# Pinning the low-part subtracts and the norms' short steps on VectorE, and looping a token-major projection over weights first

## The chip, the cores and the metric

The kernel runs on one NeuronCore of a Trainium2 chip. The time is the device time of one execution in microseconds; the number given is the median of several. The engines of the core that matter here are TensorE (PE in the profile; PEld is its weight load), VectorE (DVE), ScalarE (ACT), and the DMA queue that SyncE (SP) issues to. Each engine works through its own list of instructions in order; an instruction that waits for another engine holds up what stands behind it on its own.

## The reference

Two layers of a decoder trunk on 256 tokens with a width of 1024, all in float32. `h` is the running state, and every stage begins with an RMS norm of it.

```python
for i in range(DEPTH):                                    # DEPTH = 2
    h = h + 0.5 * swiglu(rmsnorm(h, ffn1_norm[i]), ffn1_w_gate[i], ffn1_w_up[i], ffn1_w_down[i])
    u = rmsnorm(h, mix_norm[i])
    (q, c_kv, q_idx, w_idx, k_idx, x_pool, z, xbc, dt_raw, gate_raw) = jnp.split(u @ w_in[i], offs, axis=-1)
    y_attn = dsa_attention(q, rmsnorm(c_kv, kv_norm[i]), q_idx, w_idx,
                           rmsnorm(k_idx, idx_k_norm[i]), w_uk[i], w_uv[i])
    y_pool = pool_mixer(x_pool, pool_w[i], pool_scale[i])
    y_ssd = ssd_mixer(z, xbc, dt_raw, ...)                # ends in an RMS norm too
    g_attn, g_pool, g_ssd = jnp.split(jax.nn.sigmoid(gate_raw), N_BRANCHES, axis=-1)
    h = h + (g_attn * (y_attn @ w_br_attn[i]) + g_pool * (y_pool @ w_br_pool[i])
             + g_ssd * (y_ssd @ w_br_ssd[i])) @ w_out[i]
    h = h + 0.5 * swiglu(rmsnorm(h, ffn2_norm[i]), ffn2_w_gate[i], ffn2_w_up[i], ffn2_w_down[i])
    h = h + jax.nn.sigmoid(rmsnorm(h, ple_norm[i]) @ ple_w_gate[i]) * (p[i] @ ple_w_proj[i])
return rmsnorm(h, final_norm)
```

with `rmsnorm(x, g) = x * rsqrt(mean(x*x) + EPS) * g` and `swiglu(x, g, u, d) = (silu(x @ g) * (x @ u)) @ d`. D_FF is 2816.

## The kernel before

**Products.** `h` is kept with the feature on the 128 partitions, as 8 chunks of 128 x 256 tokens. Each float32 matrix product is made of three matmuls of rounded parts (`mm3`): high of the weight by high of the state, high by low, and low by high. The parts of the state are `uh` and `ul` (`gh` and `gl` inside a feed-forward), those of the weight `whi` and `wlo`.

**Weight units.** Weights come in units of 128 x 1024 (512 KB). For each, SP issues one DMA into a `raw` buffer, ACT casts it to `whi` (L136) and DVE subtracts to get `wlo` (L137). There are four `raw` buffers and five each of `whi` and `wlo`; `unit` loads four units ahead of the one in use. So the DMA of a unit waits for the `wlo` subtract four units earlier, and the cast of a unit waits for the last matmul that reads the unit five earlier. A unit is read by 24 matmuls, except the four units `BF0` to `BF3` of the token-major part (below), which are 128 x 704 each.

**Norms.** A stage begins its matmuls on the state times the norm's gain, without the norm's factor, which is a number for each token. Meanwhile `rnorm` works out the factor: a matmul with ones over the sum of squares (L106), `rs_v` (L242), a seed and three Newton rounds on 128 x 2 numbers (L188 to L202), then the factor on a diagonal in two parts, `dh` and `dl` (L247, L248), then two matmuls with ones (L106, out of `t,onesr`), which spread it over the partitions, and an ACT copy to `rs_r` (L257). The stage's later steps (`later()`) pull the next piece of this; `gap` counts how many such pulls lie between the diagonal and the two matmuls. The results of the first matmuls are multiplied by `rs_r` as they leave their banks: in a feed-forward at L354, in the mixer at L440.

**The mixer's start.** `mix` first makes a token-major product (the units `BF0` to `BF3` are the moving side, the two halves of 128 tokens the stationary side; results in two `aux` banks; the outer loop runs over the token halves), then four index-query units `IN20` to `IN23` on the state without the norm's factor, with L440 behind them. Everything after needs the normed state: DVE makes it chunk by chunk (L449), ACT rounds it to `uh` (L175) and DVE subtracts to `ul` (L176). A second, separate norm (128 x 4 numbers, `v4` and `rk`) belongs to the attention's latent and keys.

**Order.** A list scheduler sets the order of the instructions on each engine by its own estimate of when each is ready. Matmuls are kept in program order. Everything else is free, apart from true dependences; the norm's steps have a raised priority.

## Time and profile before

| what | value |
|---|---|
| time, three runs | 1350.65, 1351.76, 1351.86 us; median 1351.76 us |
| the profiled execution: its own time | 1352.77 us |
| the profiled execution: span of the core | 1351.0 us |
| PE busy | 1316.8 us, 97% of the span |
| DVE busy | 1041.8 us, 77% |
| ACT busy | 742.8 us, 55% |
| `wlo` subtracts (L137) | 457, mean 1215 ns |
| casts to `whi` (L136) | 457, mean 1045 ns |
| weight DMA of 512 KB, issue to landing | 447, median 3.8 us |

The span runs from the first to the last instruction that the profile shows, and the execution's own time is 1.8 us longer. A share of busy time is a mean over all stages. TensorE's clock has two levels, 1.2 and 2.4 GHz; a granted clock of 1.00 in a stretch is the upper one throughout.

### The profile page before, as it was taken

The numbers are of one execution on the slowest core, as the hardware profiler recorded it, in microseconds if no ns is written. First come the engines' busy times: TensorE is split into PE (matmuls) and PEld (weight loads), VectorE is DVE, ScalarE is ACT, GpSimd is POOL, SyncE is SP. The second block draws the span as 40 slices with busy tenths as digits, with TensorE's granted clock in tenths as the row PEclk, the third lists the DMA queues.
The fourth block names the chain that finished last, engine by engine and source line by source line (L and its number), as shares of the span: only waits on it lengthen the run. The fifth ranks groups of instructions, "written<-read, shape, count | busy, mean of one in ns | idle before, by whom it ended". The sixth has DMA issues, their size and how long they took to land.

```text
span 1351.0 us, 28294 instructions
## 1 busy us (share of the span) xinstructions
PE 1316.8 (97%) x11502; PEld 1304.2 (97%) x11502; DVE 1041.8 (77%) x1971; ACT 742.8 (55%) x1209; POOL 3.4 (0%) x17
## 2 busy tenths in 40 slices
PE   7999998999999999999989999989999999999997
PEld 7999998999999999999979999989999999999997
DVE  6877658987989777766877776679789887777666
ACT  5545445656864555545545444456577646545454
POOL 0000000000000000000000000000000000000000
PEclk9999998999999999999989999989999999999999
DMA  7666645556546565666545656545565565566661
GB/s 256 196 195 192 197 155 173 179 184 206 171 155 197 194 199 190 196 193 193 190 134 189 198 191 195 167 153 171 194 197 178 171 196 192 188 198 190 196 193 48
DMA packets 72386, 248.24 MB, mean 184 GB/s; under 512 B 7937, under 2 KB 10305, under 8 KB 72257
## 3 DMA queue, kind: packets, MB, share of 16 engines
q1 hardware_dynamic: 71392, 245.17, 56.5%
q8 instruction: 90, 1.47, 0.4%
q10 hardware_dynamic: 864, 1.28, 0.3%
q14 instruction: 40, 0.32, 0.1%
HBM read 245.33 MB, written 1.08 MB: 182 GB/s over the span
## 4 chain that ended last, share of the span: by engine, by line
PE 93%; DVE 2%; DMA 1%; issue 1%; ACT 1%; SPq 0%; DVEq 0%; ACTq 0%
PE mm L159 29%; PE mm L161 29%; PE mm L160 29%; PE aux L106 3%; DMA raw<-in_w_dram 1%; ACT whi L136 1%; DVE wlo L137 1%; PE aux L109 1%; PE aux L160 1%; PE aux L159 1%; PE aux L161 1%; DMA h<-in_x_dram 0%; DVE t L449 0%; DVE rs_t L200 0%; ACT uh L179 0%
## 5 line engine op out<-in xcount | busy, mean ns | idle before, releaser
L136 ACT CAST whi<-raw 128x1024 fp32r<-128x1024 f32 (+1 forms) x457 | 475.9, 1045 | 504.2 <-issue 247.3
L159 PE MATMUL mm<-uh,whi 128*128 128x256 f32 x2560 | 714.1, 280 | 12.9 <-ACT whi L153 6.3
L137 DVE TENSOR_TENSOR wlo<-raw,whi 128x1024 fp32r<-128x1024 f32 (+1 forms) x457 | 554.4, 1215 | 219.2 <-ACT whi L136 215.2
L160 PE MATMUL mm<-ul,whi 128*128 128x256 f32 x2560 | 712.3, 279 | 6.7 <-DVE ul L176 6.7
L161 PE MATMUL mm<-uh,wlo 128*128 128x256 f32 x2560 | 711.7, 279 | 0.0
L159 PEld LDWEIGHTS mm<-uh,whi 128*128 128x128 f32 x2560 | 483.5, 190 | 17.8 <-ACT whi L153 6.3
L160 PEld LDWEIGHTS mm<-ul,whi 128*128 128x128 f32 x2560 | 485.8, 190 | 7.4 <-DVE ul L176 7.1
L161 PEld LDWEIGHTS mm<-uh,wlo 128*128 128x128 f32 x2560 | 485.1, 190 | 0.6 <-DVE wlo L154 0.2
L161 PE MATMUL mm<-gh,wlo 128*128 128x256 f32 x704 | 194.1, 276 | 0.0
L160 PE MATMUL mm<-gl,whi 128*128 128x256 f32 x704 | 194.1, 276 | 0.0
L159 PE MATMUL mm<-gh,whi 128*128 128x256 f32 x704 | 193.7, 276 | 0.0
L160 PEld LDWEIGHTS mm<-gl,whi 128*128 128x128 f32 x704 | 132.1, 188 | 0.0
L161 PEld LDWEIGHTS mm<-gh,wlo 128*128 128x128 f32 x704 | 132.1, 188 | 0.0
L159 PEld LDWEIGHTS mm<-gh,whi 128*128 128x128 f32 x704 | 131.8, 188 | 0.0
L159 PE MATMUL mm<-a,whi 128*128 128x256 f32 x256 | 70.5, 277 | 0.0
L161 PE MATMUL mm<-a,wlo 128*128 128x256 f32 x256 | 70.4, 276 | 0.0
L160 PE MATMUL mm<-a,whi 128*128 128x256 f32 x256 | 70.4, 276 | 0.0
L160 PEld LDWEIGHTS mm<-a,whi 128*128 128x128 f32 x256 | 47.9, 188 | 0.0
L159 PEld LDWEIGHTS mm<-a,whi 128*128 128x128 f32 x256 | 47.9, 188 | 0.0
L161 PEld LDWEIGHTS mm<-a,wlo 128*128 128x128 f32 x256 | 47.9, 188 | 0.0
L354 DVE TENSOR_TENSOR t<-mm,rs_r 128x256 f32<-128x256 f32 x88 | 37.3, 423 | 12.8 <-ACT rs_r L257 2.5
L359 DVE SCALAR_TENSOR_TENSOR t<-t,t 128x256 f32<-128x256 f32 x88 | 37.4, 425 | 3.1
(209 smaller groups left out, 1097.6 us busy)
## 6 DMA issues: line engine op xcount, KB each, us to landing
raw<-in_w_dram SPq DMA_DIRECT2D x447, 512.0 KB, 3.8
gh<-rates SPq DMA_DIRECT2D x16, 256.0 KB, 4.2
raw<-in_w_dram SPq DMA_DIRECT2D x8, 352.0 KB, 2.9
raw<-in_w_dram SPq DMA_DIRECT2D x4, 256.0 KB, 3.6
gh<-rates SPq DMA_DIRECT2D x8, 128.0 KB, 3.5
h<-in_x_dram SPq DMA_DIRECT2D x2, 256.0 KB, 3.9
h<-in_x_dram SPq DMA_DIRECT2D x1, 512.0 KB, 6.7
t<-in_p_dram ACTq DMA_DIRECT2D x2, 256.0 KB, 5.7
```

Source lines behind the costliest of these rows:

```text
L106: self.tc.keep_in_program_order(self.nc.tensor.matmul(*args, **kw))
L109: self.tc.keep_in_program_order(self.nc.tensor.transpose(*args))
L136: nc.scalar.copy(hi[:, :n], raw[:, :n])
L137: nc.vector.tensor_tensor(lo[:, :n], raw[:, :n], hi[:, :n].bitcast(F), op=OP.subtract)
L159: mm(ps, a[0], b[0], start=start, stop=False)
L160: mm(ps, a[0], b[1], start=False, stop=False)
L161: mm(ps, a[1], b[0], start=False, stop=stop)
L354: nc.vector.tensor_tensor(t, p1[0], r, op=OP.mult)
L359: nc.vector.scalar_tensor_tensor(g, th, 1.0, t, op0=OP.add, op1=OP.mult)
```

## The change

Three things are edited.

- `turn` gives an instruction a token, and all instructions with this token keep on their engine the order in which the program issues them. It goes on every `wlo` subtract made in `load`, and on the norms' short steps: `rs_v`, the rsqrt's steps, `dh` and `dl`. In the rsqrt of 4 numbers two of the steps in each round go without. So a `wlo` subtract can't move across such a step any more in either direction; other DVE work can still stand between.
- In the feed-forwards `gap` is 2 where it was 3, except in the kernel's first.
- In `mix` the token-major product loops over the four units outside and over the two token halves inside. The pulls of the norm's steps come after the second, third and fourth unit.

```diff
--- before.py
+++ after.py
@@ -109,6 +109,10 @@
         self.tc.keep_in_program_order(self.nc.tensor.transpose(*args))
 
 
+    def turn(self, ins):
+        self.tc.stamp_issue_order_token(ins.ins, "turn")
+
+
     AHEAD = 4
 
     def unit(self, *key):
@@ -134,7 +138,8 @@
         raw, hi, lo = self.parts()
         nc.sync.dma_start(raw[:, :n], self.ins["w"][layer, u, :, :n])
         nc.scalar.copy(hi[:, :n], raw[:, :n])
-        nc.vector.tensor_tensor(lo[:, :n], raw[:, :n], hi[:, :n].bitcast(F), op=OP.subtract)
+        self.turn(nc.vector.tensor_tensor(lo[:, :n], raw[:, :n], hi[:, :n].bitcast(F),
+                                          op=OP.subtract))
         return hi, lo
 
     def first(self, c):
@@ -185,11 +190,11 @@
         nc = self.nc
         xh = self.t([P, 8], tag="rs_h", bufs=2)
         t = self.t([P, 8], tag="rs_t", bufs=2)
-        nc.vector.tensor_scalar(t[:, :n].bitcast(I32), x.bitcast(I32), 1, None,
-                                op0=OP.logical_shift_right)
-        nc.vector.tensor_scalar(xh[:, :n], x, -0.5, None, op0=OP.mult)
-        nc.vector.tensor_scalar(y[:, :n].bitcast(I32), t[:, :n].bitcast(I32), -1, 0x5F3759DF,
-                                op0=OP.mult, op1=OP.add)
+        self.turn(nc.vector.tensor_scalar(t[:, :n].bitcast(I32), x.bitcast(I32), 1, None,
+                                          op0=OP.logical_shift_right))
+        self.turn(nc.vector.tensor_scalar(xh[:, :n], x, -0.5, None, op0=OP.mult))
+        self.turn(nc.vector.tensor_scalar(y[:, :n].bitcast(I32), t[:, :n].bitcast(I32), -1,
+                                          0x5F3759DF, op0=OP.mult, op1=OP.add))
         for _ in range(3):
             if n > 2:
                 nc.vector.tensor_tensor(t[:, :n], y[:, :n], xh[:, :n], op=OP.mult)
@@ -197,10 +202,10 @@
             else:
                 for i in range(n):
                     s = slice(i, i + 1)
-                    nc.vector.scalar_tensor_tensor(t[:, s], y[:, s], xh[:, s], y[:, s],
-                                                   op0=OP.mult, op1=OP.mult)
-            nc.vector.scalar_tensor_tensor(y[:, :n], t[:, :n], 1.5, y[:, :n],
-                                           op0=OP.add, op1=OP.mult)
+                    self.turn(nc.vector.scalar_tensor_tensor(t[:, s], y[:, s], xh[:, s],
+                                                             y[:, s], op0=OP.mult, op1=OP.mult))
+            self.turn(nc.vector.scalar_tensor_tensor(y[:, :n], t[:, :n], 1.5, y[:, :n],
+                                                     op0=OP.add, op1=OP.mult))
 
     def square(self, c, src, add=True):
 
@@ -239,14 +244,16 @@
                 for h in range(2):
                     self.mm(ps[:, h:h + 1], acc[:, h * P:(h + 1) * P], self.ones[:, :1],
                                      start=True, stop=True)
-                nc.vector.tensor_scalar(v, ps[:, :2], 1.0 / D, EPS, op0=OP.mult, op1=OP.add)
+                self.turn(nc.vector.tensor_scalar(v, ps[:, :2], 1.0 / D, EPS, op0=OP.mult,
+                                                  op1=OP.add))
                 self.rsqrt(rc, v, 2)
                 dh, dl = (self.t([P, 2, P], FR, tag="t1") for _ in range(2))
                 for h in range(2):
                     x = rc[:, h:h + 1]
-                    nc.vector.tensor_scalar(dh[:, h], self.ident, x, None, op0=OP.mult)
-                    nc.vector.scalar_tensor_tensor(dl[:, h], self.ident, x, dh[:, h].bitcast(F),
-                                                   op0=OP.mult, op1=OP.subtract)
+                    self.turn(nc.vector.tensor_scalar(dh[:, h], self.ident, x, None, op0=OP.mult))
+                    self.turn(nc.vector.scalar_tensor_tensor(dl[:, h], self.ident, x,
+                                                             dh[:, h].bitcast(F), op0=OP.mult,
+                                                             op1=OP.subtract))
             for _ in range(gap):
                 yield
             pr = self.bank("aux")
@@ -330,7 +337,7 @@
     def ffn(self, layer, u0, nxt):
         nc = self.nc
         first = layer == 0 and u0 == U_FFN1
-        _, r = self.rnorm(late=first, gap=3)
+        _, r = self.rnorm(late=first, gap=3 if first else 2)
         gh = self.a([P, KF, S], FR, "gh")
         gl = self.a([P, KF, S], FR, "gl")
         waiting = []
@@ -398,7 +405,6 @@
         u0 = self.uh, self.ul
 
 
-        wu = [self.unit(layer, U_BF + i, 2 * BF) for i in range(4)]
 
         big1 = self.a([P, KF, S], F, "gh")
         big2 = self.a([P, KF, S], F, "gl")
@@ -410,18 +416,17 @@
         sm = self.a([P, 2, 96], F, "sm")[:, :, :88]
         ki2 = self.t([P, 2, 2, 64], tag="t1")
         ss = self.t([P, 4], tag="ss", bufs=1)
-        pb = []
-        for h in range(2):
-            ts = slice(h * P, (h + 1) * P)
-            ps = self.bank("aux")
-            for k in range(KD):
-                w = wu[k // 2]
-                s = slice((k % 2) * BF, (k % 2) * BF + 344)
-                self.mm3(ps[:, :344], (u0[0][:, k, ts], u0[1][:, k, ts]),
-                         (w[0][:, s], w[1][:, s]), k == 0, k == KD - 1)
-                if k % 4 == 3:
-                    self.later()
-            pb.append(ps)
+        pb = [self.bank("aux") for _ in range(2)]
+        for i in range(4):
+            w = self.unit(layer, U_BF + i, 2 * BF)
+            for h in range(2):
+                ts = slice(h * P, (h + 1) * P)
+                for k in (2 * i, 2 * i + 1):
+                    s = slice((k % 2) * BF, (k % 2) * BF + 344)
+                    self.mm3(pb[h][:, :344], (u0[0][:, k, ts], u0[1][:, k, ts]),
+                             (w[0][:, s], w[1][:, s]), k == 0, k == KD - 1)
+            if i > 0:
+                self.later()
         for h, ps in enumerate(pb):
             nc.scalar.mul(cn[:, h], ps[:, :256], rc[:, h:h + 1])
             nc.scalar.mul(sm[:, h], ps[:, 256:344], rc[:, h:h + 1])
```

The number of matmuls, casts and subtracts and the order of the DMA issues stay as they were. Three places of the order on the engines follow. (Line numbers of the kernel after are higher by 4 to 7: L137 is L141, L200 to L202 are L205 to L207, L247 and L248 are L253 and L254, L354 is L361.)

First DVE at the start of layer 0's mixer. The norm's steps are `rs_t`, `rs_y` and the two `t` out of `ident`; `wlo_2488`, `wlo_2494`, `wlo_2500` and `wlo_2604` are the units `IN21`, `IN22`, `IN23` and `IN0`. Before:

```order
L200 SCALAR_TENSOR_TENSOR rs_t_2527<-rs_y_2479,rs_h_2526 128x1 x2
L137 TENSOR_TENSOR wlo_2488<-raw_2486,whi_2487 128x1024
L202 SCALAR_TENSOR_TENSOR rs_y_2479<-rs_t_2527,rs_y_2479 128x2
L137 TENSOR_TENSOR wlo_2494<-raw_2492,whi_2493 128x1024
L247 TENSOR_SCALAR t_372_2540<-ident,rs_y_2479 128x128 x2
L137 TENSOR_TENSOR wlo_2500<-raw_2498,whi_2499 128x1024
L137 TENSOR_TENSOR wlo_2604<-raw_2602,whi_2603 128x1024
L248 SCALAR_TENSOR_TENSOR t_373_2541<-ident,rs_y_2479,t_372_2540 128x128 x2
L794 TENSOR_TENSOR dt_x_3904<-sm_2506,cc_93 128x32
```

And after; `wlo_2549`, `wlo_2567` and `wlo_2604` are `IN22`, `IN23` and `IN0`, and `wlo_2634` is `IN32`:

```order
L205 SCALAR_TENSOR_TENSOR rs_t_2528<-rs_y_2479,rs_h_2527 128x1 x2
L207 SCALAR_TENSOR_TENSOR rs_y_2479<-rs_t_2528,rs_y_2479 128x2
L253 TENSOR_SCALAR t_367_2541<-ident,rs_y_2479 128x128
L254 SCALAR_TENSOR_TENSOR t_368_2542<-ident,rs_y_2479,t_367_2541 128x128
L253 TENSOR_SCALAR t_367_2541<-ident,rs_y_2479 128x128
L254 SCALAR_TENSOR_TENSOR t_368_2542<-ident,rs_y_2479,t_367_2541 128x128
L141 TENSOR_TENSOR wlo_2549<-raw_2547,whi_2548 128x1024
L141 TENSOR_TENSOR wlo_2567<-raw_2565,whi_2566 128x1024
L141 TENSOR_TENSOR wlo_2604<-raw_2602,whi_2603 128x1024
L799 TENSOR_TENSOR dt_x_3904<-sm_2482,cc_93 128x32
L468 TENSOR_SCALAR v_414_2771<-ss_2484 128x2
L141 TENSOR_TENSOR wlo_2634<-raw_2632,whi_2633 128x1024
```

Four subtracts stood inside the norm's steps; now that of `IN21` stands ahead of `rs_v` (not shown) and the others behind the last diagonal step. Farther on, the subtracts of the next two units, `IN1` and `IN2`, stand between the six L449 (now L454) and the first L176 (now L181); before, they stood ahead of L440, and that of `IN3` stood where they are now.

Second PE in the token-major part of layer 0: `aux_2509` and `aux_2558` are the banks of the two token halves before, `whi_2341` and `wlo_2342` are unit `BF0`, `whi_2440` is `BF3`, `mm_2601` takes `IN20`. Before, from the last matmul of the first half to the first three of the second:

```order
L161 MATMUL aux_2509<-whi_2440,ul_1745 128x344
L159 MATMUL mm_2601<-uh_1744,whi_2481 128x256
L160 MATMUL mm_2601<-ul_1745,whi_2481 128x256
L106 MATMUL aux_2522<-ones,acc_1836 128x1 x2
L159 MATMUL aux_2558<-whi_2341,uh_1744 128x344
L160 MATMUL aux_2558<-wlo_2342,uh_1744 128x344
L161 MATMUL aux_2558<-whi_2341,ul_1745 128x344
```

And after, from the fourth matmul of the part on; `aux_2485` and `aux_2486` are the banks of the halves:

```order
L164 MATMUL aux_2485<-whi_2341,uh_1744 128x344
L165 MATMUL aux_2485<-wlo_2342,uh_1744 128x344
L166 MATMUL aux_2485<-whi_2341,ul_1745 128x344
L164 MATMUL aux_2486<-whi_2341,uh_1744 128x344
L165 MATMUL aux_2486<-wlo_2342,uh_1744 128x344
L166 MATMUL aux_2486<-whi_2341,ul_1745 128x344
L164 MATMUL aux_2486<-whi_2341,uh_1744 128x344
```

The second half's matmuls on `BF0` stood behind all of the first half; now they are the seventh to the twelfth matmul of the part. The matmul of ones over the sum of squares stood behind 24 of the part's 48 matmuls and 17 matmuls on `IN20`; now it stands behind 40 of the 48 and none on `IN20`.

Third DVE at the start of layer 1's first feed-forward. `wlo_8954` and `wlo_8984` are its units `F1_6` and `F1_7`, the next two are `F1_8` and `F1_9`, and `wlo_9107` is `F1_10`. Before:

```order
L242 TENSOR_SCALAR rs_v_8861<-aux_8927 128x2
L137 TENSOR_TENSOR wlo_8954<-raw_8952,whi_8953 128x1024
L188 TENSOR_SCALAR rs_t_8932<-rs_v_8861 128x2
L190 TENSOR_SCALAR rs_h_8931<-rs_v_8861 128x2
L137 TENSOR_TENSOR wlo_8984<-raw_8982,whi_8983 128x1024
L191 TENSOR_SCALAR rs_y_8862<-rs_t_8932 128x2
L137 TENSOR_TENSOR wlo_9015<-raw_9013,whi_9014 128x1024
L200 SCALAR_TENSOR_TENSOR rs_t_8932<-rs_y_8862,rs_h_8931 128x1 x2
L137 TENSOR_TENSOR wlo_9049<-raw_9047,whi_9048 128x1024
L202 SCALAR_TENSOR_TENSOR rs_y_8862<-rs_t_8932,rs_y_8862 128x2
L137 TENSOR_TENSOR wlo_9107<-raw_9105,whi_9106 128x1024
L200 SCALAR_TENSOR_TENSOR rs_t_8932<-rs_y_8862,rs_h_8931 128x1 x2
```

And after, from the third Newton round on:

```order
L205 SCALAR_TENSOR_TENSOR rs_t_8932<-rs_y_8862,rs_h_8931 128x1 x2
L207 SCALAR_TENSOR_TENSOR rs_y_8862<-rs_t_8932,rs_y_8862 128x2
L253 TENSOR_SCALAR t_1309_8945<-ident,rs_y_8862 128x128
L254 SCALAR_TENSOR_TENSOR t_1310_8946<-ident,rs_y_8862,t_1309_8945 128x128
L253 TENSOR_SCALAR t_1309_8945<-ident,rs_y_8862 128x128
L254 SCALAR_TENSOR_TENSOR t_1310_8946<-ident,rs_y_8862,t_1309_8945 128x128
L141 TENSOR_TENSOR wlo_8954<-raw_8952,whi_8953 128x1024
L141 TENSOR_TENSOR wlo_8984<-raw_8982,whi_8983 128x1024
L141 TENSOR_TENSOR wlo_9037<-raw_9035,whi_9036 128x1024
L141 TENSOR_TENSOR wlo_9067<-raw_9065,whi_9066 128x1024
L361 TENSOR_TENSOR t_1319_9016<-mm_8865,rs_r_8860 128x256
L141 TENSOR_TENSOR wlo_9107<-raw_9105,whi_9106 128x1024
```

The subtracts of `F1_6` to `F1_10` stood singly between the norm's steps; now the steps from `rs_v` to the last diagonal step stand in one piece, four subtracts follow, and then comes the first L361 (before: L354).

## Rows read from the trace of the kernel before

**Rows 1.** The page: span; busy us, share and instructions of each engine.
```profile
span 1351.0 us, 28294 instructions
...
PE 1316.8 (97%) x11502; PEld 1304.2 (97%) x11502; DVE 1041.8 (77%) x1971; ACT 742.8 (55%) x1209; POOL 3.4 (0%) x17
```

**Rows 2.** Windows: length, busy PE, PEld, DVE, ACT, POOL, PEclk, DMA share, GB/s.
```profile
200.00:240.00 40.00, 34.36 (x282) 33.83 (x281) 32.62 (x78) 24.53 (x45) 0.00 (x0) 0.91 0.51 169
219.00:230.00 11.00, 10.87 (x80) 10.87 (x81) 7.29 (x23) 3.46 (x6) 0.00 (x0) 0.83 0.24 73
240.00:300.00 60.00, 60.00 (x545) 59.67 (x544) 56.00 (x135) 37.94 (x59) 0.59 (x2) 1.00 0.55 173
887.00:898.00 11.00, 11.00 (x78) 11.00 (x79) 6.69 (x22) 3.21 (x6) 0.00 (x0) 0.78 0.19 63
```

**Rows 3.** PE timeline, mixer of layer 0: start, us, instruction, [idle before <-releaser].
```profile
212.60 0.28 PE L161 MATMUL mm<-uh,wlo 128*128 128x256 f32 x1
214.97 0.62 PE L159 MATMUL mm<-uh,whi 128*128 128x256 f32 x3 [2.10 <-ACT uh L175]
219.13 0.58 PE L160 MATMUL mm<-ul,whi 128*128 128x256 f32 x1 [3.54 <-DVE ul L176]
219.51 0.41 PE L161 MATMUL mm<-uh,wlo 128*128 128x256 f32 x1
```

**Rows 4.** Timeline of PE, start of the token-major part of layer 0.
```profile
193.49 0.32 PE L159 MATMUL aux<-whi,uh 128*128 128x344 f32 x1
193.65 0.32 PE L160 MATMUL aux<-wlo,uh 128*128 128x344 f32 x1
```

**Rows 5.** Timeline of ACT, start of layer 0's mixer.
```profile
200.88 3.90 ACT L136 CAST whi<-raw 128x1024 fp32r<-128x1024 f32 x4 [5.45 <-issue]
...
211.93 0.37 ACT L257 COPY rs_r<-aux 128x256 f32<-128x256 f32 x1
```

**Rows 6.** Timeline of DVE, start of layer 0's mixer.
```profile
199.78 0.16 DVE L242 TENSOR_SCALAR rs_v<-aux 128x2 f32<-128x2 f32 x1 [3.12 <-PE aux L106]
...
201.96 1.23 DVE L137 TENSOR_TENSOR wlo<-raw,whi 128x1024 fp32r<-128x1024 f32 x1
...
204.31 0.48 DVE L247 TENSOR_SCALAR t<-ident,rs_y 128x128 fp32r<-128x128 f32 x2
204.70 2.36 DVE L137 TENSOR_TENSOR wlo<-raw,whi 128x1024 fp32r<-128x1024 f32 x2
206.97 0.61 DVE L248 SCALAR_TENSOR_TENSOR t<-ident,rs_y,t 128x128 fp32r<-128x128 f32 x2
...
213.88 2.46 DVE L449 SCALAR_TENSOR_TENSOR t<-h,cc,rs_r 128x256 f32<-128x256 f32 x6
...
216.92 1.22 DVE L137 TENSOR_TENSOR wlo<-raw,whi 128x1024 fp32r<-128x1024 f32 x1
...
218.66 1.09 DVE L176 TENSOR_TENSOR ul<-t,uh 128x256 fp32r<-128x256 f32 x3
```

**Rows 7.** Timeline of PE, start of layer 1's mixer.
```profile
883.00 0.62 PE L159 MATMUL mm<-uh,whi 128*128 128x256 f32 x3 [1.85 <-ACT uh L175]
886.79 0.58 PE L160 MATMUL mm<-ul,whi 128*128 128x256 f32 x1 [3.17 <-DVE ul L176]
```

**Rows 8.** Timeline of PE, start of layer 1's first feed-forward.
```profile
688.52 0.28 PE L161 MATMUL mm<-uh,wlo 128*128 128x256 f32 x1
694.55 1.01 PE L106 MATMUL aux<-t,onesr 128*128 128x256 f32 x2 [5.76 <-DVE t L247]
696.49 0.58 PE L159 MATMUL mm<-uh,whi 128*128 128x256 f32 x1 [0.92 <-DVE t L354]
```

**Rows 9.** Timeline of DVE, start of layer 1's first feed-forward.
```profile
684.33 0.15 DVE L242 TENSOR_SCALAR rs_v<-aux 128x2 f32<-128x2 f32 x1
...
691.63 1.22 DVE L137 TENSOR_TENSOR wlo<-raw,whi 128x1024 fp32r<-128x1024 f32 x1 [1.28 <-ACT whi L136]
...
696.01 0.42 DVE L354 TENSOR_TENSOR t<-mm,rs_r 128x256 f32<-128x256 f32 x1 [1.08 <-ACT rs_r L257]
```

## The prediction

> **What bounds the kernel now.** The page comes first: PE is busy for 1316.8 of 1351.0 us [rows 1]. So only PE's idle time and the time in which it runs at the lower clock can be won. Second come windows of PE's busy time along the span: they are full except in seven places: the start and the end of the kernel, which no edit touches, a small gap at each second feed-forward, and three larger ones, at the start of layer 0's mixer (34.36 of 40 us, clock 0.91 [rows 2]), of layer 1's first feed-forward and of layer 1's mixer. Third, PE's timeline there, where the reader is to see the gaps and their releasers.
>
> In layer 0's mixer PE stops after the matmul at 212.60, runs three at 214.97, and waits 3.54 us more, for `ul`, till 219.13 [rows 3]. At 219.51 a matmul takes 0.41 us where 0.28 is usual, and the granted clock from 219 to 230 is 0.83 [rows 2, 3]: 17% of 11 us, 1.9 us, is lost on top of 5.6 idle. Layer 1's mixer shows the same shape: restarts at 883.00 and 886.79, idle 1.85 and 3.17 [rows 7], then a clock of 0.78 over 11 us, 2.4 us lost [rows 2]. In the feed-forward PE stops after 688.52, is idle 5.76 before the two spreading matmuls and 0.92 behind them, and starts anew at 696.49 [rows 8]. Fourth, who is late: DVE and ACT. In the mixer four `wlo` subtracts run between the first Newton round and the last diagonal step: `rs_v` is at 199.78, L248 only at 206.97 [rows 6]; ACT stood still for 5.45 us and then casts four units in a row at 200.88 [rows 5], because it waited for the buffers of the `BF` units, whose last reader was the second token half.
>
> **The change, part by part.**
>
> *Loop order.* A token-major matmul starts 0.16 us after the one ahead [rows 4]. `BF0` is released after 12 of them, 193.49 + 12 x 0.16 = 195.4; the casts of `IN21` to `IN0` then run from there as units come free (one every 1.9 us), in time ACT spent idle, and are done by 202.5 instead of 204.8. No instruction is added. The price: the ones matmul stands behind 40 of them, 193.49 + 40 x 0.16 = 199.9, so `rs_v` comes at about 200.4 instead of 199.78, 0.6 later.
>
> *Pins, mixer of layer 0.* From `rs_v` to the first subtract between is 2.2 us [rows 6]; one L202 (0.2) and four diagonal steps (0.48 and 0.61 for two each, overlapping: 1.0) remain, so the norm in one piece takes about 3.3 us: 200.4 + 3.3 = 203.7. Spreading and the copy follow (1.1 us with a 0.37 us copy [rows 5]) and PE is then inside `IN21`, at about 206.5: `rs_r` at 207.4 instead of 211.93. On DVE three subtracts at 1.15 each (two took 2.36 with their overlap [rows 6]) end at 207.1, `IN32` and small steps at 208.5. Then L445 (0.6) and six L454 (2.46 [rows 6]): 211.5. Now the two pinned subtracts, `IN1` and `IN2`: their raw slots come free with those of `IN22` and `IN23` (204.8, 206.0), a transfer takes 3.8 us by the page and a cast 1.05, so they're castable at 209 to 211, and ACT has the `uh` casts beside them; they end at 213.8. L181 for the key rows (0.6) and the first `ul` (0.35) bring 214.8, PE 214.9. Against 219.13 this is 4.2 us. PE runs dry at 212.9 as before, so one gap of 2.0 us is left.
>
> *The clock.* The row of 214.97 is a restart after 2.10 us idle, and its three matmuls take 0.62 us together, as fast as ever; the restart after a second gap of 3.54 is the slow one [rows 3]. In layer 1 it is the same with 1.85 and 3.17 [rows 7]. So with one gap of 2.0 I count the lost 1.9 us as won back, though no row shows a single gap of 2 us followed by a long run. The Trainium skill, "TensorE: Matmul & The Clock Gate", section "What's actually happening", says the monitor that sets the clock runs freely and that the count of slow matmuls after a start differs from run to run; by it the term could be 0 in either mixer, and the sum 4.3 us less. The trace agrees in so far as 1.9 and 2.4 differ.
>
> *Mixer of layer 1.* Its `rs_v` lies as far from its restart as in layer 0, and its restart is at 886.79. The chain of layer 0 moved by the distance of the two first restarts (883.00 - 214.97 = 668.0 [rows 3, 7]) gives 214.9 + 668.0 = 882.9, at most 883.3 if counted from `rs_v`: 3.6 us, and 2.4 of clock.
>
> *Pins and gap, feed-forward of layer 1.* `rs_v` starts at 684.33 [rows 9], behind the subtract of `F1_5`, and still does. In one piece the norm ends at 687.6. PE is busy till 688.8, so spreading is over before `gap` could matter: its 2 for 3 is worth nothing here, since DVE comes last. Four pinned subtracts follow: 4 x 1.15 = 4.6, to 692.2. That of `F1_9` needs the slot of `F1_5` (free at 684.3), a transfer and a cast (5 to 6 us): 690.1, just ahead of its turn at 691.0; before, a subtract waited 1.28 us for its cast and the norm stood behind it [rows 9]. L361 takes 0.42 (696.01 to a restart at 696.49 before): 692.6. PE starts at 692.7 instead of 696.49: 3.8 us. The gap is then 3.9 us, near the 3.17 and 3.54 that were followed by slow matmuls, so no clock is won; 0 to 2 us is the bound.
>
> *The other norms.* PE doesn't idle at the norms of the scan and of the embedding, so nothing can be won there; at the second feed-forwards one or two subtracts stand ahead of L361 before and after. I count them at 0 each; the bounds are half a subtract's 1.2 us [rows 6] either way.
>
> *Given back.* From 240 to 300 us DVE is busy for 56.00 of 60 while PE never idles [rows 2]. PE now reaches this stretch 6 us earlier, DVE has to as well; it had 3.7 us idle from 219 to 230 [rows 2] and as much again in the ten after. Five `wlo` buffers and the banks cover the rest. Bounds 0 and 2 us per layer; I take 0.7, as no row shows PE short there.
>
> Sum: 4.2 + 1.9 + 3.6 + 2.4 + 3.8 = 15.9, less 1.4: 14.5 us. The profiled execution took 1352.77 us, 1.0 above the median of 1351.76 (1.8 of it outside its span); a gain inside the span carries over, so 1351.76 - 14.5 = **1337.3 us**.
>
> **Rivals.**
> - *The clock stays low behind the shorter gap.* For it: both second restarts ran slow, and nothing shows what a first gap alone does to the matmuls some microseconds later [rows 2, 3, 7]. Against: both first restarts were fast. Loses 4.3: 1341.6.
> - *`ul` waits for weights instead.* The pinned `IN1` and `IN2` now stand ahead of `ul`, so a late transfer stops the state itself. For it: a subtract waiting for its cast held the norm 1.28 us [rows 9]. Against: by the sum they have 1 to 2 us in hand. If transfers take 2 us more, both mixers restart 2 us later and slow: 4.0 + 4.3 less, 1345.6.
> - *More than counted.* The feed-forward's clock comes back too (2.0), nothing is given back (1.4): 1333.9.
> - *No change that shows.* DVE bounds each mixer's second part, and all that the mixers win is idle time there; the feed-forward's 3.8 is halved by a late `F1_9`: 1349.9.
> - *Slower.* The pins work everywhere, ten norms in all. A norm in one piece keeps subtracts waiting for 3.3 us, longer still when `rs_v` waits for PE: everything with a token stands behind it. Where PE has less weight in hand than that, it stops. For the seven norms outside the three places the gain of 14.5 is eaten once each costs 2.1 us; at 3.3 each the time is 1351.8 - 14.5 + 23.1 = 1360.4. Against: in the mixer, with DVE at its fullest, the norm ran uninterrupted for 2.2 us while PE went on [rows 6]; a matmul takes 60.00 / 545 = 0.11 us [rows 2], so a unit's 24 last 2.6 us and the four units made ahead 10.6. The Trainium skill, "DVE: scalar operands, raw-bit mode, write accounting and state across instructions", section "Flops that outlive an instruction", calls DVE's queue one in-order queue, which is why a pinned wait holds all behind it; the trace agrees [rows 9].
>
> **How the numbers follow.** As summed 0.50, low clock 0.17, late weights 0.10, more 0.12, no change 0.06, slower 0.05. A measurement of this kernel tells about 0.2%, 2.7 us, from no change. Faster by more than that: 0.89; within: 0.06; slower: 0.05. The lower end of the range, 1331, is the case of more less half a subtract at five of the other norms (3.0); the upper end, 1346, takes in the late weights. Left out are 0.11 above and little below.
>
> **What would show it.** After, the casts start at 195.4 without the 5.45 us of idle; `rs_v` to the last diagonal step takes 3.3 us with no subtract between; `rs_r` is near 207.4; PE has one gap of about 2 us in each mixer, released by `ul`, at a clock of 1.00 after it; in the feed-forward a gap of 3.9 us released by L361, behind four subtracts. Wrong would be: a gap released by a cast or transfer of `IN1` or `IN2`, a clock of 0.8 after a 2 us gap, idle PE between 240 and 300 us or at the scan's norm.

## The result and the profile after

The changed kernel took 1337.18 us (median of four runs, 1336.48 to 1340.05), the kernel before 1351.81 us (four runs, 1350.65 to 1352.81). The ratio is 0.9896 with a 95% interval of 0.9879 to 0.9913: 14.6 us faster, where 14.5 were forecast. The profiled execution is the longest of the four (1340.05 us, span 1338.3).

The page of the changed kernel, against [rows 1]: span; busy us, share and instructions of each engine.

```profile
span 1338.3 us, 28287 instructions
...
PE 1312.2 (98%) x11502; PEld 1300.5 (97%) x11502; DVE 1040.4 (78%) x1971; ACT 742.9 (56%) x1209; POOL 3.4 (0%) x17
```

PE is busy 4.6 us less for the same 11502 matmuls (fewer of them at the lower clock), and its idle time falls from 34.2 to 26.1 us. DVE's and ACT's work is the same within 1.4 us; only its order is new. Between the two profiled executions the span shrinks by 12.7 us, 1.9 less than the medians do.

PE's timeline of the changed kernel, against [rows 3], [rows 7] and [rows 8].

```profile
212.88 0.62 PE L164 MATMUL mm<-uh,whi 128*128 128x256 f32 x3 [0.27 <-ACT uh L180]
214.90 0.39 PE L165 MATMUL mm<-ul,whi 128*128 128x256 f32 x1 [1.39 <-DVE ul L181]
...
215.99 0.42 PE L164 MATMUL mm<-uh,whi 128*128 128x256 f32 x1
...
440.89 0.38 PE L164 MATMUL mm<-uh,whi 128*128 128x256 f32 x1 [0.94 <-ACT uh L180]
...
684.34 0.39 PE L106 MATMUL aux<-t,onesr 128*128 128x256 f32 x2
688.59 0.58 PE L164 MATMUL mm<-uh,whi 128*128 128x256 f32 x1 [3.86 <-DVE t L361]
688.97 0.41 PE L165 MATMUL mm<-ul,whi 128*128 128x256 f32 x1
...
875.94 0.39 PE L165 MATMUL mm<-ul,whi 128*128 128x256 f32 x1 [1.79 <-DVE ul L181]
```

In layer 0's mixer two stops of 2.10 and 3.54 us have become 0.27 and 1.39; the second is still released by `ul`. In layer 1's mixer 1.85 and 3.17 have become one of 1.79. In the first feed-forward of layer 1 the stop ahead of the two spreading matmuls (5.76 us) is gone, they run at 684.34 without waiting, and the one behind them, released by L361, has grown from 0.92 to 3.86. At 440.89 (and at 1100.14 in layer 1, 0.76 us) there is a stop that the kernel before did not have.

Windows over the mixers and the stretch behind, against [rows 2]: length, busy PE, PEld, DVE, ACT, POOL, PEclk, DMA share, GB/s.

```profile
200.00:240.00 40.00, 38.34 (x325) 37.73 (x324) 34.95 (x85) 24.50 (x49) 0.00 (x0) 0.96 0.51 168
215.00:226.00 11.00, 11.00 (x83) 11.00 (x84) 8.82 (x27) 2.79 (x5) 0.00 (x0) 0.84 0.33 114
240.00:300.00 60.00, 60.00 (x540) 59.74 (x538) 55.05 (x133) 36.48 (x55) 0.58 (x2) 1.00 0.63 187
876.00:887.00 11.00, 11.00 (x96) 11.00 (x97) 10.42 (x30) 5.22 (x9) 0.00 (x0) 1.00 0.44 122
```

From 200 to 240 PE has 38.34 busy us instead of 34.36. Behind the stop in layer 1 the clock is now 1.00; behind the one in layer 0 it is 0.84: the restart at 214.90 runs at full speed, and 1.1 us later the matmuls start to follow each other at 0.22 instead of 0.11 us, for 15 of them.

ACT's timeline, against [rows 5], and farther on the cast of the `ple` input `p` ahead of the second feed-forward.

```profile
195.38 1.05 ACT L140 CAST whi<-raw 128x1024 fp32r<-128x1024 f32 x1 [0.19 <-ACT t L218]
197.28 1.05 ACT L140 CAST whi<-raw 128x1024 fp32r<-128x1024 f32 x1 [0.85 <-PE aux L166]
...
206.86 0.37 ACT L264 COPY rs_r<-aux 128x256 f32<-128x256 f32 x1 [0.89 <-PE aux L106]
...
210.95 1.06 ACT L140 CAST whi<-raw 128x1024 fp32r<-128x1024 f32 x1 [1.52 <-DMA raw<-in_w_dram]
...
433.25 0.34 ACTq L1082 DMA_DIRECT2D t<-in_p_dram  x1
438.96 0.62 ACT L180 CAST t<-t 128x512 fp32r<-128x512 f32 x1 [4.67 <-DMA t<-in_p_dram]
...
440.44 0.40 ACT L180 CAST uh<-t 128x256 fp32r<-128x256 f32 x1
```

The same transfer and casts in the kernel before:

```profile
437.59 0.34 ACTq L1077 DMA_DIRECT2D t<-in_p_dram  x1
438.54 0.40 ACT L175 CAST uh<-t 128x256 fp32r<-128x256 f32 x1
...
443.38 0.62 ACT L175 CAST t<-t 128x512 fp32r<-128x512 f32 x1 [2.03 <-DMA t<-in_p_dram]
```

The 5.45 us of standing still are gone: the casts of these units run one by one from 195.38, the three after the first each released by a matmul of the token-major part (`PE aux L166`), and `rs_r` is there at 206.86 instead of 211.93. At 433.25 ACT issues the transfer of `p`, and the next thing in its list is the cast of `p`, which waits 4.67 us for it; a weight cast and a cast of `uh` stand behind it, and PE's stop at 440.89 is released by that cast of `uh`. In the kernel before, a cast of `uh` and a weight cast stood between the issue and the cast of `p`.

DVE's timeline, against [rows 6] and [rows 9].

```profile
200.11 0.16 DVE L247 TENSOR_SCALAR rs_v<-aux 128x2 f32<-128x2 f32 x1 [2.42 <-PE aux L106]
...
203.37 0.35 DVE L254 SCALAR_TENSOR_TENSOR t<-ident,rs_y,t 128x128 fp32r<-128x128 f32 x1
203.64 3.49 DVE L141 TENSOR_TENSOR wlo<-raw,whi 128x1024 fp32r<-128x1024 f32 x3
...
209.02 2.47 DVE L454 SCALAR_TENSOR_TENSOR t<-h,cc,rs_r 128x256 f32<-128x256 f32 x6
211.39 2.37 DVE L141 TENSOR_TENSOR wlo<-raw,whi 128x1024 fp32r<-128x1024 f32 x2
...
214.41 1.10 DVE L181 TENSOR_TENSOR ul<-t,uh 128x256 fp32r<-128x256 f32 x3
...
680.06 0.15 DVE L247 TENSOR_SCALAR rs_v<-aux 128x2 f32<-128x2 f32 x1
...
683.31 0.35 DVE L254 SCALAR_TENSOR_TENSOR t<-ident,rs_y,t 128x128 fp32r<-128x128 f32 x1
683.58 4.62 DVE L141 TENSOR_TENSOR wlo<-raw,whi 128x1024 fp32r<-128x1024 f32 x4
688.12 0.42 DVE L361 TENSOR_TENSOR t<-mm,rs_r 128x256 f32<-128x256 f32 x1
```

The norm runs in one piece, from 200.11 to 203.72 (3.6 us; before it took 7.8, from 199.78 to the end of L248 at 207.58), and the subtracts stand behind it in rows of three and four.

### The profile page after: what moved, and what is told of

The parts are those of the page before. It is cut to its first block, busy times and chain, and to the rows that moved or that the text cites. A ratio compares the mean times of both kernels' runs of the same rounds, so it can differ in the third digit from the quotient of the medians.

```text
span 1338.3 us, 28287 instructions
## 1 busy us (share of the span) xinstructions
PE 1312.2 (98%) x11502; PEld 1300.5 (97%) x11502; DVE 1040.4 (78%) x1971; ACT 742.9 (56%) x1209; POOL 3.4 (0%) x17
## 4 chain that ended last, share of the span: by engine, by line
PE 93%; DVE 4%; DMA 1%; issue 1%; ACT 0%; DVEq 0%; SPq 0%; ACTq 0%
PE mm L164 29%; PE mm L166 29%; PE mm L165 29%; PE aux L106 3%; DVE wlo L141 1%; PE aux L164 1%; PE aux L165 1%; PE aux L166 1%; DMA t<-in_p_dram 1%; PE aux L109 1%; DMA h<-in_x_dram 0%; DVE t L454 0%; DVE rs_t L205 0%; DMA raw<-in_w_dram 0%; ACT whi L140 0%
## 5 line engine op out<-in xcount | busy, mean ns | idle before, releaser
L141 DVE TENSOR_TENSOR wlo<-raw,whi 128x1024 fp32r<-128x1024 f32 (+1 forms) x457 | 552.1, 1214 | 207.5 <-ACT whi L140 202.8
L166 PE MATMUL mm<-uh,wlo 128*128 128x256 f32 x2560 | 710.3, 278 | 0.2 <-DVE wlo L141 0.2
L166 PEld LDWEIGHTS mm<-uh,wlo 128*128 128x128 f32 x2560 | 483.9, 189 | 1.0 <-DVE wlo L141 0.4
L166 PE MATMUL mm<-gh,wlo 128*128 128x256 f32 x704 | 194.1, 276 | 0.0
L166 PEld LDWEIGHTS mm<-gh,wlo 128*128 128x128 f32 x704 | 132.2, 188 | 0.0
L166 PE MATMUL mm<-a,wlo 128*128 128x256 f32 x256 | 69.9, 277 | 0.0
L166 PEld LDWEIGHTS mm<-a,wlo 128*128 128x128 f32 x256 | 47.6, 188 | 0.0
L361 DVE TENSOR_TENSOR t<-mm,rs_r 128x256 f32<-128x256 f32 x88 | 37.3, 423 | 10.3 <-PE mm L166 1.3
L180 ACT CAST gh<-t 128x256 fp32r<-128x256 f32 x88 | 35.1, 399 | 9.0 <-DVE t L366 9.0
```

The lines of the kernel that those rows point to most:

```text
L141: self.turn(nc.vector.tensor_tensor(lo[:, :n], raw[:, :n], hi[:, :n].bitcast(F), op=OP.subtract))
L166: mm(ps, a[1], b[0], start=False, stop=stop)
L180: self.nc.scalar.copy(hi, src)
L361: nc.vector.tensor_tensor(t, p1[0], r, op=OP.mult)
```

## The experiments

To compare traces part by part, the span is cut at the first matmul of each feed-forward's second product (`mm<-gh,whi` on PE's timeline; 133.65, 583.10, 801.92 and 1251.46 us in the kernel before). "Start" is the first feed-forward of layer 0 up to its cut; "mixer 0" holds layer 0's mixer and the first part of its second feed-forward, "ffn1" the way through layer 1's first feed-forward, "mixer 1" layer 1's mixer and the first part of its second feed-forward; the rest (99.3 to 99.9 us) hardly differs. A star marks a mixer whose restart was followed by matmuls at half speed. The segments are those of the one profiled execution; the time is the median of all of that kernel's runs.

| kernel | start | mixer 0 | ffn1 | mixer 1 | time |
|---|---|---|---|---|---|
| before | 133.65 | 449.45* | 218.82 | 449.54* | 1351.81 |
| after | 133.41 | 446.35* | 214.71 | 444.51 | 1337.18 |
| e1_again | 131.51 | 444.91 | 213.96 | 444.54 | 1335.88 |
| e5_again2 | 131.81 | 446.57* | 214.75 | 444.88 | 1339.30 |
| e4_gap3 | 131.81 | 446.60* | 214.74 | 444.74 | 1339.49 |
| e6_gap3b | 131.59 | 444.51 | 213.98 | 444.96 | 1336.90 |
| e2_loop_only | 134.41 | 449.14* | 218.91 | 449.66* | 1350.41 |
| e3_pins_only | 133.63 | 450.62* | 213.98 | 451.48* | 1349.86 |
| e7_first_product | 131.72 | 444.52* | 210.05 | 444.44 | 1332.62 |
| e9_first_product_again | 131.99 | 443.70 | 210.09 | 446.15* | 1333.18 |
| e8_first_product_p | 134.18 | 442.93 | 210.06 | 444.74* | 1332.95 |
| e10_first_product_p_again | 134.35 | 443.00 | 210.09 | 444.76* | 1331.03 |
| e11_in_two_late | 131.74 | 443.76 | 210.09 | 444.63 | 1331.10 |
| e12_in_one_late | 131.69 | 443.28 | 210.07 | 443.15 | 1329.65 |

**The halves of the change.** e2 keeps the new loop and takes the tokens away; e3 keeps the tokens and takes the loop away. Both have `gap` 3.

```diff
 # e2_loop_only
     def turn(self, ins):
-        self.tc.stamp_issue_order_token(ins.ins, "turn")
+        return ins
 # e3_pins_only
+        wu = [self.unit(layer, U_BF + i, 2 * BF) for i in range(4)]
...
-        for i in range(4):
-            w = self.unit(layer, U_BF + i, 2 * BF)
-            for h in range(2):
...
+        for h in range(2):
...
+            for k in range(KD):
+                w = wu[k // 2]
```

> The new loop order alone: no tokens, gap 3. Worked out from its order on VectorE with the traced durations: casts from 195.4 as in the changed kernel, but the subtracts of IN23, IN0 and IN32 stand inside the norm's steps and IN1 and IN2 ahead of L445, so the first ul ends at about 216.9 in layer 0 (changed kernel 214.8, before 219.0): 2.2 us for each mixer, 0 in layer 1's first feed-forward, clock term 0 to 2 each: 1347 us, 1343 to 1348. Rival, the mixers' gain is the freed weight buffers alone: first ul near 214.9 in both and 1342. Rival, the loop order is worth nothing without the tokens: 1351.8.

> The tokens alone, on the old loop order, gap 3. In the mixer the pinned order puts the subtracts of IN21 to IN23 ahead of rs_v, and their casts still wait for the second token half (200.9 on), so the norm starts only at about 205 and ends at 208.5; four subtracts follow, then L447: first ul at about 217.2, 1.9 us won for each mixer, 3.8 in layer 1's first feed-forward (PE gap 3.9 us released by L361): 1344 us, 1342 to 1346. Rival, the tokens carry the whole gain: 1337. Rival, tokens without the loop order hold the mixer's norm back by more than they save: slower than 1348.

The loop alone took 1350.41 us (11 runs), ratio 0.9988 (0.9980 to 0.9997) against 1352.16 us of the kernel before beside it; the tokens alone 1349.86 us (11 runs), ratio 0.9981 (0.9972 to 0.9990). Both are far from the 1347 and 1344 us that were expected of them, and far less than the whole; nearest came the rivals by which the loop is worth nothing without the tokens and the tokens without the loop take more than 1348. By the table the loop alone wins nothing in either mixer (0.3 and -0.1 us); the tokens alone win 4.8 us in the feed-forward and lose 1.2 and 1.9 in the mixers. Of these losses 0.3 and 0.5 are a later restart; the rest is about the stops of 0.95 and 1.50 us at the cast of `p`, which e3 has and e2 has not: the new stop at `p` comes with the tokens. DVE's timeline of e2 shows why the loop alone is empty.

```profile
201.11 0.16 DVE L247 TENSOR_SCALAR rs_v<-aux 128x2 f32<-128x2 f32 x1 [0.52 <-PE aux L106]
201.26 1.23 DVE L141 TENSOR_TENSOR wlo<-raw,whi 128x1024 fp32r<-128x1024 f32 x1
...
203.62 1.23 DVE L141 TENSOR_TENSOR wlo<-raw,whi 128x1024 fp32r<-128x1024 f32 x1 [0.27 <-ACT whi L140]
...
206.31 1.22 DVE L141 TENSOR_TENSOR wlo<-raw,whi 128x1024 fp32r<-128x1024 f32 x1
207.45 0.61 DVE L254 SCALAR_TENSOR_TENSOR t<-ident,rs_y,t 128x128 fp32r<-128x128 f32 x2
```

The casts came early (from 196.38), but so did the subtracts behind them: `rs_v` starts 1.3 us later than before (0.8 of it from the start), three subtracts still stand inside the norm, and its last step ends at 208.06, where it ended at 207.58 before. In e3 it is the other way round; ACT's and DVE's timelines:

```profile
200.86 3.91 ACT L140 CAST whi<-raw 128x1024 fp32r<-128x1024 f32 x4 [5.45 <-issue]
...
213.53 0.37 ACT L264 COPY rs_r<-aux 128x256 f32<-128x256 f32 x1
...
201.94 3.50 DVE L141 TENSOR_TENSOR wlo<-raw,whi 128x1024 fp32r<-128x1024 f32 x3 [5.29 <-ACT whi L140]
205.35 0.15 DVE L247 TENSOR_SCALAR rs_v<-aux 128x2 f32<-128x2 f32 x1
...
208.59 0.35 DVE L254 SCALAR_TENSOR_TENSOR t<-ident,rs_y,t 128x128 fp32r<-128x128 f32 x1
```

The norm is in one piece, but the pinned subtracts ahead of it wait for casts, which wait for the buffers of the token-major part as before (5.45 us), so `rs_v` starts at 205.35 and `rs_r` comes at 213.53, 1.6 us later than before the change. Each half removes one of two waits in series, and the other takes its place; only both together shorten the mixer.

**The same kernel again, and `gap`.** e1 and e5 are the changed kernel unedited; e4 and e6 give it the old `gap`.

```diff
-        _, r = self.rnorm(late=first, gap=3 if first else 2)
+        _, r = self.rnorm(late=first, gap=3)
```

> The changed kernel once more, unedited, for a second profile. In the first profile the clock fell in layer 0's mixer about 1 us after a restart behind a 1.4 us gap (15 matmuls at the low rate) and did not fall in layer 1's mixer behind 1.8 us; that execution took 1340.05 us where the others took 1336.5 to 1337.5. If the low clock there comes and goes from execution to execution: about 1337 us, the same gaps (1.4 and 1.8 us before the first ul, 3.9 us before the first L361), and slow matmuls in another place or none in the mixers. Rival, the low clock belongs to the gap: again some 15 slow matmuls in layer 0's mixer, and none in layer 1's.

> The changed kernel with gap 3 in every feed-forward: only two matmuls of the spreading stand later on PE. My step says gap is worth nothing since VectorE comes last (four subtracts between the norm and the first L361): same as the changed kernel within 0.5 us, 1337. Rival, gap 2 carries part of the feed-forward's gain: about 1339 to 1341, with the gap in layer 1's first feed-forward released by the copy to rs_r and not by L361.

> The changed kernel once more, unedited, beside the next one: 1336.5 us (1335 to 1338.5), as in its two sets of runs so far. By every theory the stops of TensorE in the trace are those of before (about 1.8 us in either mixer, 3.86 us in the second layer's first feed-forward, some 0.9 us where the ple input is cast), and the matmuls at half clock behind them come and go.

> The changed kernel with the gap of 3 kept in all norms, once more. If the gap is worth nothing, as predicted, it agrees with the unedited kernel beside it within 0.1% (1336.5 +- 1.5 us) and the 2.8 us between their medians in the first pair were drift of the runs; if it is worth something, it is again 2 to 3 us slower (1339 us) and its stops in the feed-forwards are longer.

Unedited it took 1335.88 us (1335.00 to 1338.34, ratio 0.9880, 0.9867 to 0.9894) and 1339.30 us (1336.39 to 1339.63, ratio 0.9899, 0.9884 to 0.9914); with `gap` 3, 1339.49 us (ratio 0.9905, 0.9890 to 0.9921) and 1336.90 us (ratio 0.9889, 0.9874 to 0.9903). The first pair spoke for a gap worth 3.6 us, the second for one worth -2.4; the two kernels can't be told apart, and in the table e4 has the segments of e5, e6 those of e1. What differs inside each pair is the clock. Of the 16 executions of these four kernels the seven with a mean granted clock of 0.995 to 0.997 took 1335.00 to 1337.35 us and the nine with 0.993 or 0.994 took 1338.26 to 1340.76, with either `gap` in both groups. Windows of e1 and of e5 over the 11 us from the restart in layer 0's mixer:

```profile
213.00:224.00 11.00, 11.00 (x96) 11.00 (x97) 8.95 (x28) 3.61 (x6) 0.00 (x0) 1.00 0.38 122
```

```profile
213.00:224.00 11.00, 10.73 (x79) 10.73 (x80) 8.83 (x28) 2.77 (x5) 0.00 (x0) 0.84 0.34 127
```

The same program, after stops of 1.83 and 1.78 us: 96 matmuls at 1.00 in one execution, 79 at 0.84 in the other, 15 of them at half speed.

**The order behind the norm in the feed-forward.** L361 (f1 = 0) frees the first bank; in the changed kernel it stands behind four subtracts.

```diff
-                    nc.vector.tensor_tensor(t, p1[0], r, op=OP.mult)
+                    i = nc.vector.tensor_tensor(t, p1[0], r, op=OP.mult)
+                    if f1 == 0:
+                        self.turn(i)
```

> The first product with rs_r of each feed-forward (line 361, f1 = 0) joins the token order too, which puts it two subtracts earlier on VectorE (behind two of the four subtracts that ran ahead of it, 4.62 us for the four). Theory, that the order of the queue alone sets this stop: in the second layer's first feed-forward the stop of 3.86 us becomes about 1.6 us, and up to 2 us of half-clock matmuls behind it go too, so 1333 us (1331.5 to 1335). Rival, that the stop is set by the norm's result or that TensorE next waits for the two subtracts put behind: the gain returns as a new stop on a wlo, and the time stays at 1336.5 us.

> The kernel with line 361's first product in the token order, once more, beside the next three: 1332.6 us (1331.5 to 1334), with stops of some 1.6 to 1.8 us in the mixers and 1.6 us in the second layer's first feed-forward.

1332.62 us (1332.36 to 1333.62), ratio 0.9857 (0.9840 to 0.9873), and 1333.18 us, ratio 0.9863 (0.9848 to 0.9878). PE's and DVE's timelines of e7:

```profile
680.07 2.35 DVE L141 TENSOR_TENSOR wlo<-raw,whi 128x1024 fp32r<-128x1024 f32 x2
682.35 0.42 DVE L361 TENSOR_TENSOR t<-mm,rs_r 128x256 f32<-128x256 f32 x1
682.68 2.35 DVE L141 TENSOR_TENSOR wlo<-raw,whi 128x1024 fp32r<-128x1024 f32 x2
...
682.82 0.39 PE L164 MATMUL mm<-uh,whi 128*128 128x256 f32 x1 [1.59 <-DVE t L361]
```

With two subtracts ahead of L361 instead of four the stop is 1.59 instead of 3.86 us, no slow matmuls follow it, and the segment is 4.7 us shorter than in `after` (3.9 shorter than in e1): 2.27 of it is the stop, the rest the matmuls at half speed. No new stop comes for the two subtracts put behind, as the rival had it. So 2.27 of the 3.86 us were DVE's order alone; that the last 1.59, with two subtracts still ahead, are so too was not tried.

**The fetch of `p`.** In addition to e7's edit, the transfer of `p` is issued on GpSimd's queue ahead of the mixer's last stage.

```diff
         self.new_u()
+        self.pt = self.t([P, 2, S])
+        nc.gpsimd.dma_start(self.pt, self.ins["p"][layer])
         for cs in ((0, 1), *((c,) for c in range(2, 8))):
...
-            pt = self.t([P, 2, S])
-            nc.scalar.dma_start(pt, self.ins["p"][i])
...
-            self.split(*self.p, pt)
+            self.split(*self.p, self.pt)
```

> As the last one, and the ple input p is fetched through GpSimd's queue ahead of the mixer's last stage instead of through ScalarE's queue right ahead of its cast. Theory, that the new stops of 0.94 and 0.76 us ahead of the second feed-forwards come from ScalarE standing 4.7 us at that cast with a cast of uh queued behind it: both stops go, 1.7 us less than the kernel beside it, so 1331.5 us (1329.5 to 1333.5). Rival, that the uh cast was late for another reason (VectorE's t): the stops stay and the time is that of the kernel beside it.

> The kernel with both edits, once more: by the trace the two stops at the ple input's cast (1.0 and, in other runs, 0.8 to 1.1 us) are gone. Theory, that they are worth their own length: 1.0 to 2.0 us below the kernel beside it, 1331 us (1330 to 1332.5). Rival, that the time they cost is made up by later cover: equal to the kernel beside it within 0.5 us.

1332.95 us (1331.19 to 1333.60, ratio 0.9855, 0.9840 to 0.9870) and 1331.03 us (1329.31 to 1333.59, ratio 0.9847, 0.9829 to 0.9865). Beside e7 and e9 the time says nothing clear: e8 is 0.3 us above its neighbour, e10 2.2 below, and the intervals overlap. The traces do: ACT's cast of `p` no longer waits, and neither trace has a stop ahead of a second feed-forward, where e9 has 0.50 and 1.03 us. ACT's timeline of e10:

```profile
436.28 0.61 ACT L180 CAST t<-t 128x512 fp32r<-128x512 f32 x1
436.80 0.40 ACT L180 CAST uh<-t 128x256 fp32r<-128x256 f32 x1
```

Between e9 and e10, with the same stars, the mixers' segments are 0.7 and 1.4 us shorter, about the length of the stops. What the edit wins there these two traces lose again at the start, which is 2.4 us longer though nothing in it was edited (below). The stop also depends on how long the transfer takes: in e7's layer 0 it landed 4.1 us after its issue instead of 5.7, and TensorE did not stop. The edit both moves the issue (to 417 us) and changes its queue; which of the two matters was not tried.

**The order ahead of `ul` in the mixer.** In addition to e7's edit, the index-query loop fetches two (e11) or three (e12) units ahead; behind it the number is 4 again.

```diff
+        self.AHEAD = 2                     # e12_in_one_late: 3
         for i in range(0, 4, 2):
             ps = self.in_pair(layer, T_QI + i, u0)
...
+        self.AHEAD = 4
         xs = self.a([P, 8, S], F, "uh", 2)
```

> Fetch the weights two instead of four units ahead in the index-query loop of the mixer only, which puts the subtracts of IN1 and IN2 behind the first ul on VectorE (2.35 us of subtracts leave the place ahead of ul and come back behind the short steps, some 6 us later). Theory, that the stop at ul is set by those two subtracts alone: it goes (1.8 to 0 us in either mixer), but TensorE is then through IN0 after 2.7 us and waits about 3.7 us for IN1's low part, so each mixer loses about 2 us and the time is 1336.5 us (1335 to 1340), slower than the kernel beside it. Rival, that the cast of IN0 to IN2 or the norm sets ul: the stop at ul stays and the loss is 5 us and more.

> The same with three units ahead: only IN2's subtract (1.2 us) goes behind the first ul. Theory: the stop at ul falls from about 1.8 to 0.6 us, and a new one of about 1.6 us comes at IN2, two units of 2.7 us later; net 0.4 us slower per mixer, 1333.5 us (1332 to 1335). Rival: IN2's low part is in time and the mixers gain 1.2 us each, 1330.5 us.

e11 took 1331.10 us (1329.73 to 1331.86), ratio 0.9845 (0.9830 to 0.9859), where 1336.5 and a loss were expected; e12 took 1329.65 us (1329.01 to 1329.98), ratio 0.9834 (0.9820 to 0.9848), the rival's 1330.5 rather than the theory's 1333.5. PE's timeline of e11:

```profile
217.89 0.38 PE L164 MATMUL mm<-uh,whi 128*128 128x256 f32 x1 [0.57 <-ACT whi L140]
```

And of e12:

```profile
212.04 0.39 PE L165 MATMUL mm<-ul,whi 128*128 128x256 f32 x1 [0.77 <-DVE ul L181]
...
865.38 0.39 PE L165 MATMUL mm<-ul,whi 128*128 128x256 f32 x1 [0.62 <-DVE ul L181]
```

The first half of the expectation held: without `IN1` and `IN2` ahead of it `ul` is in time and the stop is gone; without `IN2` it is 0.77 and 0.62 us. The second half failed. I had let TensorE run through `IN0` alone (2.7 us) before it needs `IN1`; but `IN0` is woven with `IN32`, whose subtract is not among the moved ones, so 48 matmuls run first, 5.4 us. The low part of `IN1` is then ready in time; e11's stop of 0.57 us waits for a cast, and e12 has none there. Neither has a mixer with matmuls at half speed. Of the 3.5 us between e9 and e12, 2.0 are the shorter stops at `ul` (1.92 and 1.44 in e9); the half-speed matmuls of e9's layer 1 are about the rest. e12 is the fastest of all kernels here, 22.5 us below the kernel before; e8's fetch of `p` was not joined to it.

## Why the prediction was right

**Loop order.** Forecast: casts from 195.4, `rs_v` at 200.4. Measured: 195.38 and 200.11. Right, with its price.

**Pins, mixer of layer 0.** Norm in one piece 3.3 us, measured 3.6; `rs_r` at 207.4, measured 206.86 with a length of 0.37; the two pinned subtracts to end at 213.8, measured 213.76; PE at 214.9, measured 214.90. Since this execution is 0.24 us ahead at the start, the term is 4.0 us for 4.2. e2 and e3 show that it belongs to the loop and the pins together.

**The clock.** 1.9 and 2.4 us were counted as won back in full. That was the mis-sized term. With a stop of 1.4 to 1.9 us the half-speed matmuls came in layer 0's mixer in 4 of 9 traces (after, e4, e5, e7) and in layer 1's in 3 of 9 (e8 to e10), where they came in all six mixers of the kernels with the long stops (before, e2, e3). They cost about 1.7 us when they come (446.35 to 446.60 us against 444.51 to 444.91 with the `p` stop in all of them). In the profiled execution the prediction's own sign of being wrong, a low clock behind a short stop, is there: 0.84 in layer 0's mixer. The rival of a clock that stays low is thus true in some executions and false in others of the same program. The step behind the term was misread: the prediction laid the fall to the second, longer stop, since the matmuls behind the first ran fast. Windows of the kernel before:

```profile
213.00:215.90 2.90, 0.62 (x3) 0.41 (x3) 2.90 (x9) 2.75 (x6) 0.00 (x0) 1.00 0.85 291
216.00:219.00 3.00, 0.00 (x0) 0.00 (x0) 3.00 (x7) 1.39 (x3) 0.00 (x0) 0.50 0.08 31
```

The granted clock had fallen to 0.50, the lower level, 1.0 us behind the first restart (214.97) and long before the second (219.13); layer 1's fell between 884.9 and 885.1, ahead of the restart at 886.79. In `after` too it fell 1.0 us behind the restart at 214.90. So the fall did not need the length of the second stop, of which 0.4 us had passed in layer 0, and a single shorter stop was no safeguard. The Trainium skill, "TensorE: Matmul & The Clock Gate", section "What's actually happening", says that the monitor behind the clock runs freely, so that the number of slow matmuls at a kernel's start differs between runs of one kernel; behind a stop in the middle e1 and e5 differ in the same way, with 0 and 15.

**Mixer of layer 1.** The restart moved from 886.79 to 875.94, of which 7.45 us had been won ahead of it (801.92 to 794.47): 3.4 for a forecast of 3.6.

**Feed-forward of layer 1.** Four subtracts behind the norm (4.62 us as forecast), L361 last, a stop of 3.86 for 3.9, no clock won: right. The restart came 4.6 us earlier, net of what was won ahead (7.90 - 3.34), for 3.8: `rs_v` came 0.9 sooner than counted on. Some 0.5 is lost again to more slow matmuls, and the segment is 4.1 us shorter. e7 shows that 2.27 us of this stop were the order's and were there to be won.

**`gap`.** Counted at nothing; e4 and e6 against `after`, e1 and e5 agree.

**The other norms.** Counted at 0 within half a subtract. At the second feed-forwards the stop falls from 0.47 to 0.25 and 0.21 us. Apart from the new stops at `p`, taken up next, PE stopped nowhere else, so the slower rival found no place.

**Given back.** Counted at 0.7 us a layer, for the stretch from 240 to 300 us. There PE has no idle time (60.00 of 60), and DVE is less busy than before (55.05 for 56.00). 0.94 and 0.76 us were lost elsewhere, where ACT stands at the cast of `p`. So the size came out by luck and the reason did not: I had not looked at what ACT issues for itself. Before, the cast of `p` waited 2.03 us with nothing late behind it; the tokens alone (e3) bring the new stops, through the order of ACT's list, in which nothing was pinned.

**The start.** Not in the sum, as no edit touches it. In the profiled execution it is 0.24 us shorter, but in e1, e4 to e7, e9, e11 and e12 it is 1.7 to 2.1 us shorter. It stands against the part of the clock that did not come back. Only one execution of each set was traced, so how the two divide in the medians is not shown; that 14.5 met 14.6 so closely is in part luck.

By segments, the profiled execution won 0.2 + 3.1 + 4.1 + 5.0 + 0.2 us, where the terms gave 0, 5.4, 3.8, 5.3 and 0. It is the slowest of its set: its mean granted clock is 0.993, that of the other three 0.995 or 0.996.

**`ul` waits for weights.** This rival had the right place and no price in the forecast kernel: the two subtracts were fed in time (the cast at 210.95 waited 1.52 us for its transfer and was done, at 212.01, half a microsecond before the second of the two subtracts began). But that they stand ahead of `ul` is what PE waits for there: without them the stop is gone (e11), and e12 wins most of it.

## What to carry to other kernels

Where two engines' queues feed a stop in series (here casts that wait for buffers, and a norm split by subtracts), undo each half of a change before crediting either: alone each was worth nothing in the mixer, together 3 to 5 us per layer. A pinned order is only as good as the position of the one instruction that frees the waiting engine; when a stop remains, count what stands ahead of its releaser in the queue and move what TensorE needs last (some 4 us for one token, 3.5 more for one number, with what the clock gave back in both). When counting how long work can be put off, count all units woven into TensorE's stream, not the one that bears the next name.

## What the runs showed of the hardware

TensorE's clock can fall behind a short stop, and whether it does is not settled by the program. In e1 and e5, after the same stop of 1.8 us, the granted clock stayed at 1.00 in one execution and was 0.84 over 11 us in the other. In the seven mixers where it fell behind a stop of 1.4 to 1.9 us the first slow matmul came 0.5 to 1.3 us after a restart at full speed, not at the restart. Behind the stops of 0.57 to 0.77 us of e11 and e12 it did not fall (four of four).

The start of the kernel took 133.4 to 134.4 us in six traces (before, after, e2, e3, e8, e10) and 131.5 to 132.0 in eight, though the first instructions on SP, ACT and DVE are the same in all. Much of the difference is TensorE's speed early on. PE's windows of `after` and e1, two executions of one program (busy PE, PEclk, DMA share, GB/s):

```profile
14.50:17.50 3.00, 3.00 (x15) 0.50 0.67 201
```

```profile
14.50:17.50 3.00, 3.00 (x28) 1.00 0.75 218
```

In this stretch the six with the long start make 13 to 15 matmuls, the eight others 25 to 29. (Of the six only `after` has its granted clock on record this early; in the other five the record starts at 18 to 19 us, and a window ahead of that reads 1.00.) In five of the six the slowest of the three loads of the input landed 6.5 to 7.1 us after its issue, in the eight with the short start 6.0 to 6.3. But in `after` too it landed 6.1 us after its issue, and its start is long all the same, where e1's and e5's, of the same program, are short; so late loads are not the whole cause, and what it is stays open. A difference of 2 us between two traces can come from there alone, so segments tell more than the total.
